# A decoder layer on one core: the residual and the row scaling ahead of the MLP moved to GpSimd

## The chip, the cores and the metric

The kernel runs on one core of a Trainium2 chip. The core has five engines with instruction queues of their own: TensorE (PE in the profile, with its weight loads as PEld), VectorE (DVE), ScalarE (ACT), GpSimd (POOL) and SyncE (SP), which issues most DMAs. Each engine works through its queue in order. An instruction that needs another engine's result waits for a semaphore, and everything behind it on its engine waits too. The metric is the device time of one launch in microseconds.

## The reference

One layer of a decoder, for a prompt of 256 tokens and for 8 samples of one token each, with 2048 channels in float32. Cut to the part around the change:

```python
x = x + gt1 * rmsnorm(out, p['g_post_mix'][l])          # the residual after the mixers

h2 = rmsnorm(x, p['g_pre_mlp'][l]) * (1.0 + sc2) + sh2  # input of the MLP
y2 = jnp.square(jax.nn.relu(h2 @ p['w_mlp_up'][l])) @ p['w_mlp_down'][l]
x = x + gt2 * rmsnorm(y2, p['g_post_mlp'][l])
```

`out` is the output projection of the three mixers (2048 by 2048). `w_mlp_up` is 2048 by 8192 and `w_mlp_down` 8192 by 2048. A row of `x` is one token, and both norms go over a row: each needs one factor per token. The kernel calls them `r1` (from the norm of `out`) and `r2` (from the norm of the new `x`).

## The kernel before

Every large product is computed in three passes (L602, L603, L604) over operands that are split into a high and a low part. `split` does this with a cast on ACT (L109) and a subtraction on DVE (L106), both for weights (`whi`, `wlo`) and for activations (`h2h`, `h2l`). The moving operand has 264 columns: 256 prompt tokens and 8 sample columns. Weights arrive as blocks of 128x1024 by SP's DMAs and are split up to two granules ahead of use.

The change lies at the seam between the output projection and the MLP. At this place the order of PE, DVE and ACT is written out by hand (`manual_schedule`, L1448); POOL's order there follows the order of the code. The steps, in order:

- `norms` and `rstd_sqrt` compute `r1` (ready at L199). `x1` holds the prompt's rows of the input, `og` the gated rows of `out`, as four tiles of 128x1024 each: two halves of tokens (`t`) by two halves of channels.
- POOL handles the samples' columns: two products (L1455, L1456), the residual of the samples (L1483, L1484), and their modulation (L1485, L1499, L1500) into `xa`.
- A chain of small 128x10 operations on DVE (L100, L1489, L103, L1492, L195 to L199) gives `r2` without forming the new rows first. From `r1` and `r2` come four diagonal matrices `dg` (L1497 on DVE, L1498 on ACT).
- The channels go into the MLP in four quarters of 512. `quad(0)` forms the first quarter on PE, by matmuls of the rows against `dg` (L1534, L1535), so that it needs no residual. `quad(1)` to `quad(3)` need the finished residual: `residual(q)` adds `r1*og` to `x1` in place on DVE (L1508, one 128x512 instruction for each `t`), ACT scales the rows by `r2` into two tiles named `gt` (L1515), and PE transposes them (L1532). `put_quad` then modulates the transposed quarter on DVE and ACT (L1545, L1547) and splits it (L109, L106).
- `begin_up` multiplies the quarters by the first 512 columns of `w_mlp_up`. After the granules for k = 0, 4 and 8 it issues `quad(1)`, `quad(2)` and `quad(3)`; after those for k = 2 and 6 it issues `residual(2)` and `residual(3)`, and at the end `residual(0)`. `residual(1)` stands right behind `quad(0)`. A granule here is 24 matmuls.
- The tiles `gt` have two buffers for all users. `dg` takes one of them, and each quarter's two scaled tiles take both.

Of the kernel before, what the change touches and what calls it, by code (L numbers as in the profile page):

```python
# [7 lines left out]
F32 = mybir.dt.float32  # L8
F32R = mybir.dt.float32r
I32 = mybir.dt.int32  # L10
AF = mybir.ActivationFunctionType
ALU = mybir.AluOpType
# [3 lines left out]
P = 128  # L16
D = 2048
KT = D // P
NP = 256
NS = 8  # L20
NT = NP + NS
# [36 lines left out]
def hybrid_step_kernel(  # L58
# [9 lines left out]
    V, S, T = nc.vector, nc.scalar, nc.tensor  # L68
# [13 lines left out]
    def nm(s):  # L82
        uid[0] += 1
        return f"{s}_{uid[0]}"

    def blk(shape=None, dt=F32):
        shape = shape or [P, 4, NT]
        return blkp.tile(shape, dt, tag="b", name=nm("b"))

    def sm(shape=None):  # L90
        return psm.tile(shape or [P, 512], F32, tag="sm", name=nm("sm"))

    def tmp(shape, tag, bufs=2):
        return tp.tile(shape, F32, tag=tag, name=nm(tag), bufs=bufs)
# [13 lines left out]
    def split(src, hi, lo):  # L108
        S.copy(hi, src)  # L109
        sub(lo, src, hi.bitcast(F32))  # L110

    order = tc.manual_schedule(engines={mybir.EngineType.PE, mybir.EngineType.SP, mybir.EngineType.Pool})
# [77 lines left out]
    def rstd_sqrt(ms, scale, out):  # L190

        n, w = out.shape
        xx, aa = tmp([P, 16], "sx")[0:n, 0:w], tmp([P, 16], "sa")[0:n, 0:w]
        S.activation(out, ms, AF.Sqrt, scale=scale, bias=eps)
        V.tensor_scalar(xx, ms, scale, EPS, ALU.mult, ALU.add)  # L195
        V.reciprocal(out, out)
        mul(aa, out, out)
        V.scalar_tensor_tensor(aa, aa, -0.5, xx, ALU.mult, ALU.mult)
        V.scalar_tensor_tensor(out, aa, 1.5, out, ALU.add, ALU.mult)  # L199
# [453 lines left out]
    def background():  # L653

        now[0] += 1
        while later and later[0][0] < now[0]:
            later.pop(0)[1]()
        bg.pump(rate[0])
        bs.pump(rate[1])
        wait = max([now[0] + 1 - AGE - x[0] for x in levels + samples] + [0])  # L660
        if wait and any(x[1][0].i == 2 for x in samples):
            wait += 2
        if rounds.due() and (wait or now[0] >= rounds.at + rounds.pace) or wait >= SLOT_WAIT:
            slot()
        rounds.tick()

    def new_acc():
        return pmm.tile([P, 2, 512], F32, tag="mm", name=nm("mm"))
# [229 lines left out]
    order = tc.manual_schedule(engines={mybir.EngineType.PE, mybir.EngineType.Pool})  # L898
# [460 lines left out]
    x1 = [[blk([P, 1024]) for _ in range(2)] for _ in range(2)]  # L1359
# [6 lines left out]
    def gated(m, src, Gv):  # L1366

        k = 2 * m
        sq = tmp([P, 2, NT], "vt")
        g = tmp([P, 2, NT], "gt")  # L1370
        if m < 7:
            S.activation(sq, src, AF.Square)
        else:
            S.activation(sq[:, 0, :], src[:, 0, :], AF.Square)
        V.tensor_scalar(g[:, 1, 0:NP], src[:, 1, 0:NP], Gv[:, k + 1, 0:1], None, ALU.mult)
        if m == 7:
            S.activation(sq[:, 1, :], src[:, 1, :], AF.Square)
        S.activation(g[:, 0, 0:NP], src[:, 0, 0:NP], AF.Copy, scale=Gv[:, k, 0:1])
        if m == 0:
            add(sqacc, sq[:, 0, :], sq[:, 1, :])  # L1380
        else:
            add(sqacc, sqacc, sq[:, 0, :])
            add(sqacc, sqacc, sq[:, 1, :])
        mul(gs[:, k:k + 2, :], src[:, :, NP:NT], Gv[:, k:k + 2, 1:NC])
        return g
# [26 lines left out]
    def norms():  # L1412

        ps = sm([P, 2 + NS])
        for t in range(2):
            T.matmul(ps[:, t:t + 1], sqacc[:, t * P:(t + 1) * P], ones[:, 0:1], start=True, stop=True)
        T.matmul(ps[:, 2:2 + NS], ones, sqacc[:, NP:NT], start=True, stop=True)
        r = tmp([P, 2 + NS], "nr", 1)
        rstd_sqrt(ps, 1.0 / D, r)
        return r  # L1420

    order = tc.manual_schedule(engines={mybir.EngineType.PE})
    order.__enter__()
    og = [[blk([P, 1024]) for _ in range(2)] for _ in range(2)]
# [20 lines left out]
    V.scalar_tensor_tensor(A2, mod[:, 4 * KT:5 * KT, :], 1.0, gpre2T.unsqueeze(2).to_broadcast([P, KT, NC]), ALU.add, ALU.mult)  # L1445
    B2 = mod[:, 3 * KT:4 * KT, :]
    order.__exit__(None, None, None)
    order = tc.manual_schedule(engines={mybir.EngineType.PE, mybir.EngineType.DVE, mybir.EngineType.Activation})  # L1448
    order.__enter__()
    Q = nc.gpsimd  # L1450
    rounds.steps(2)
    g = gated(7, z, G1)

    sp = tmp([P, 2, KT, NS], "os2", 1)
    Q.tensor_tensor(sp[:, 0], gs, xsT, op=ALU.mult)  # L1455
    Q.tensor_tensor(sp[:, 1], gs, gs, op=ALU.mult)  # L1456
    r1 = norms()

    pt = new_acc()
    for t in range(2):  # L1460
# [21 lines left out]
    xa = tmp([P, KT, NS], "xsn", 1)  # L1482
    Q.tensor_tensor(gs, gs, r1[:, 2:2 + NS].unsqueeze(1).to_broadcast([P, KT, NS]), op=ALU.mult)  # L1483
    Q.tensor_tensor(xsT, xsT, gs, op=ALU.add)  # L1484
    Q.tensor_tensor(xa, xsT, A2[:, :, 1:NC], op=ALU.mult)  # L1485

    q = tmp([P, 2 + NS], "rr", 1)
# [5 lines left out]
    r2 = tmp([P, 2 + NS], "rr0", 1)  # L1493
    rstd_sqrt(q, 1.0 / D, r2)
    dg = tmp([P, 4, P], "gt")
    for t in range(2):
        V.tensor_scalar(dg[:, t, :], ident, r2[:, t:t + 1], None, ALU.mult)  # L1497
        S.activation(dg[:, 2 + t, :], d1[:, t, :], AF.Copy, scale=r2[:, t:t + 1])  # L1498
    Q.tensor_tensor(xa, xa, r2[:, 2:2 + NS].unsqueeze(1).to_broadcast([P, KT, NS]), op=ALU.mult)  # L1499
    Q.tensor_tensor(xa, xa, B2[:, :, 1:NC], op=ALU.add)  # L1500
    h2h, h2l = [blk(dt=F32R) for _ in range(4)], [blk(dt=F32R) for _ in range(4)]

    def residual(q):

        cs = slice(q % 2 * 512, q % 2 * 512 + 512)
        for t in range(2):
            x = x1[t][q // 2][:, cs]
            V.scalar_tensor_tensor(x, og[t][q // 2][:, cs], r1[:, t:t + 1], x, ALU.mult, ALU.add)  # L1508

    def quad(q):  # L1510

        if q > 0:
            rows = [tmp([P, 4, P], "gt") for _ in range(2)]
            for t in range(2):
                S.activation(rows[t].rearrange("p k f -> p (k f)"), x1[t][q // 2][:, q % 2 * 512:q % 2 * 512 + 512], AF.Copy, scale=r2[:, t:t + 1])  # L1515
        hs, ls = (h[q][:, :, NP:NT] for h in (h2h, h2l))
        Q.tensor_copy(hs, xa[:, 4 * q:4 * q + 4, :])
        Q.tensor_tensor(ls, xa[:, 4 * q:4 * q + 4, :], hs.bitcast(F32), op=ALU.subtract)
        for i2 in range(2):
            if q > 0:  # L1520
                ps = sm([P, 2, NP])
            vt = tmp([P, 2, NT], "vt")
            for i in range(2):
                c0 = q % 2 * 512 + (2 * i2 + i) * P
                if q == 0:
                    pk = sm([P, NP])
                else:
                    pk = ps[:, i, :]
                for t in range(2):
                    o = pk[:, t * P:(t + 1) * P]  # L1530
                    if q > 0:
                        T.transpose(o, rows[t][:, 2 * i2 + i, :], ident)  # L1532
                    else:
                        T.matmul(o, x1[t][0][:, c0:c0 + P], dg[:, t, :], start=True, stop=False)  # L1534
                        T.matmul(o, og[t][0][:, c0:c0 + P], dg[:, 2 + t, :], start=False, stop=True)  # L1535
                if q == 0:
                    put_quad(q, i2, i, pk, vt)
            if q > 0:
                for i in range(2):
                    put_quad(q, i2, i, ps[:, i, :], vt)  # L1540

    def put_quad(q, i2, i, src, vt):
        k = 4 * q + 2 * i2 + i
        if i == 0 and (q == 0 or i2 == 0):
            V.tensor_scalar(vt[:, i, 0:NP], src, A2[:, k, 0:1], B2[:, k, 0:1], ALU.mult, ALU.add)  # L1545
        else:
            S.activation(vt[:, i, 0:NP], src, AF.Identity, scale=A2[:, k, 0:1], bias=B2[:, k, 0:1])  # L1547
        if q == 0 or i == 1:
            a = i if q == 0 else 0
            js = slice(2 * i2 + a, 2 * i2 + i + 1)  # L1550
            split(vt[:, a:i + 1, 0:NP], h2h[q][:, js, 0:NP], h2l[q][:, js, 0:NP])

    quad(0)
    residual(1)

    rate[:] = (0.0, 0.0)
    rounds.pace, rounds.batch = 5, 2
# [3 lines left out]
    def begin_up():  # L1561

        accs = [new_acc(), new_acc()]
        for k in range(0, KT, 2):
            granule(w_mlp_up[0], 0, 2, 0, 2 * CW, accs, h2H, h2L, k, k == 0, k + 2 == KT)
            if k % 4 == 0 and k + 4 < KT:
                quad(k // 4 + 1)
            elif k + 6 < KT:
                residual(k // 4 + 2)
            elif k + 2 == KT:  # L1570
                residual(0)
            if k >= 8:
                background()
        return [a[:, :, 0:NT] for a in accs]
# [47 lines left out]
    order = tc.manual_schedule(engines={mybir.EngineType.PE})  # L1622
# [99 lines left out]
```

## Time and profile before

| | |
|---|---|
| median of 3 runs | 1942.22 us (1941.23 to 1944.57) |
| span of the profiled execution | 1942.9 us, 42324 instructions |
| PE busy | 1903.4 us (98%) |
| PEld busy | 1812.1 us (93%) |
| DVE busy | 1186.1 us (61%) |
| ACT busy | 1006.5 us (52%) |
| POOL busy | 83.9 us (4%) |
| mean granted clock of PE | 0.994 |

The profile is one execution, and it gives the span from the first to the last instruction as that execution's own time; nothing outside the span is listed for it. The span is 0.7 us above the median of the three runs and inside their spread. Rows of the timeline begin with the start in us from the span's start and the duration in us; a bracket at the end names the idle time before the row and what ended it. Rows of the waits name who waited for whom: the sum in us, how often, and the longest.

### The profile page before, as it was taken

Reading aid. Unit: us, or ns where it says so; the run is one execution under the profiler, and the core shown is the slowest. Engines: PE = TensorE matmul, PEld = TensorE weight load, DVE = VectorE, ACT = ScalarE, POOL = GpSimd, SP = SyncE. Lnnn points to the kernel's source line nnn. Section 1 sums busy time; section 2 is a strip of 40 time slices with the busy share of each in tenths; the row PEclk is TensorE's granted clock in tenths of the full one; section 3 lists DMA queues with packets and bytes.
Section 4 is the critical chain, followed back from the end, with each engine's and each line's share of the span. In section 5 each row is a group of like instructions: output and inputs, shape, how many; then the busy total and the mean of one; then the engine's idle time right before and its main releaser. Section 6 shows DMA issues by size and latency. Waiting matters only on the chain.

```text
span 1942.9 us, 42324 instructions
## 1 busy us (share of the span) xinstructions
PE 1903.4 (98%) x17080; PEld 1812.1 (93%) x17080; DVE 1186.1 (61%) x2103; ACT 1006.5 (52%) x1825; POOL 83.9 (4%) x142
## 2 busy tenths in 40 slices
PE   6999999998999999999999999999999999999998
PEld 5989999988999998999999988999999999999997
DVE  4566667686578695565555666545556555555665
ACT  5444454665666765544444556444444545454444
POOL 1000000001001112200000010000000000000000
PEclk9999999999999999999999999999999999999999
DMA  9897786688588688987777846776566555555552
GB/s 317 299 337 247 249 287 213 214 250 276 175 262 290 214 258 283 306 266 249 253 256 233 300 129 195 229 226 199 178 182 184 179 180 184 177 183 182 179 183 99
DMA packets 339380, 442.06 MB, mean 228 GB/s; under 512 B 14930, under 2 KB 281024, under 8 KB 339184
## 3 DMA queue, kind: packets, MB, share of 16 engines
q1 hardware_dynamic: 329120, 409.62, 65.5%
q0 software_dynamic: 8992, 28.48, 4.6%
q8 instruction: 134, 2.20, 0.5%
q10 hardware_dynamic: 1072, 1.25, 0.2%
q14 instruction: 62, 0.51, 0.1%
HBM read 427.60 MB, written 11.70 MB: 226 GB/s over the span
## 4 chain that ended last, share of the span: by engine, by line
PE 95%; DMA 2%; issue 1%; ACT 1%; DVE 1%; POOL 0%; SPq 0%; ACTq 0%; DVEq 0%; POOLq 0%
PE mm L602 29%; PE mm L603 29%; PE mm L604 28%; PE ada L342 3%; PE ada L274 1%; PE sm L633 1%; PE sm L780 1%; DMA raw<-in_w_in_dram 1%; PE sm L640 0%; DMA b<-in_x_prompt_dram 0%; DMA vbc<-vs_d 0%; DVE wlo L106 0%; DMA b<-in_w_ada_dram 0%; ACT gt L1515 0%; PE sm L1176 0%
## 5 line engine op out<-in xcount | busy, mean ns | idle before, releaser
L602 PE MATMUL mm<-b,whi 128*128 128x264 f32 x4624 | 1326.6, 287 | 7.5 <-ACT b L109 3.5
L603 PE MATMUL mm<-b,whi 128*128 128x264 f32 x4624 | 1317.8, 285 | 0.8 <-DVE b L106 0.8
L604 PE MATMUL mm<-b,wlo 128*128 128x264 f32 x4624 | 1314.5, 284 | 1.4 <-issue 0.7
L106 DVE TENSOR_TENSOR wlo<-raw,whi 128x512 fp32r<-128x512 f32 x1136 | 775.5, 689 | 572.0 <-ACT whi L109 570.0
L109 ACT CAST whi<-raw 128x512 fp32r<-128x512 f32 x1136 | 695.4, 618 | 730.6 <-PE mm L603 654.5
L602 PEld LDWEIGHTS mm<-b,whi 128*128 128x128 f32 x4624 | 872.3, 189 | 49.1 <-issue 26.2
L604 PEld LDWEIGHTS mm<-b,wlo 128*128 128x128 f32 x4624 | 872.5, 189 | 2.2 <-DVE wlo L106 1.1
L603 PEld LDWEIGHTS mm<-b,whi 128*128 128x128 f32 x4624 | 872.2, 189 | 1.4 <-DVE b L106 1.3
L103 DVE TENSOR_TENSOR b<-b,mm 128x528 f32<-128x528 f32 (+1 forms) x137 | 95.7, 700 | 42.7 <-PE mm L604 42.7
L1057 DVE SCALAR_TENSOR_TENSOR st<-vbc,b,st 128x128 f32<-128x128 f32 (+1 forms) x96 | 34.1, 389 | 51.1 <-DMA vbc<-vs_d 44.2
L1055 ACT ACTIVATE st<-st,fs 128x128 f32<-128x128 f32 (+1 forms) x96 | 37.0, 430 | 53.0 <-DMA st<-in_state_hgrn_dram 27.0
L274 PE MATMUL ada<-b,cT 128*32 128x256 f32 (+1 forms) x640 | 35.7, 361 | 7.2 <-DMA b<-in_w_ada_dram 7.0
L342 PE MATMUL ada<-araw,cT 128*32 128x512 f32 x296 | 39.9, 601 | 0.0
L274 PEld LDWEIGHTS ada<-b,cT 128*32 128x32 f32 x640 | 18.2, 115 | 19.7 <-issue 6.4
L100 DVE TENSOR_TENSOR b<-b,b 128x512 f32<-128x512 f32 (+1 forms) x47 | 34.1, 740 | 1.4 <-ACT b L1165 0.9
L1058 POOL DMA_DIRECT2D out_dram<-st x32 | 23.5, 735 | 156.6 <-DVE st L1057 150.8
L342 PE MATMUL ada<-b,cT 128*32 128x512 f32 x216 | 26.2, 593 | 0.0
L106 DVE TENSOR_TENSOR b<-gt,b 128x528 fp32r<-128x528 f32 x32 | 22.7, 708 | 3.9 <-ACT whi L109 0.9
L106 DVE TENSOR_TENSOR b<-b 128x1024 f32<-128x1024 f32 (+1 forms) x24 | 24.3, 1016 | 0.0
L109 ACT CAST whi<-araw 128x512 fp32r<-128x512 f32 x20 | 12.4, 621 | 20.7 <-PE mm L603 19.0
L100 DVE TENSOR_TENSOR gt<-vt 128x528 f32<-128x528 f32 x32 | 22.4, 701 | 0.9 <-ACT vt L1581 0.9
L1587 ACT ACTIVATE b<-vt 128x528 fp32r<-128x528 f32 x32 | 20.7, 647 | 1.0
(339 smaller groups left out, 825.2 us busy)
## 6 DMA issues: line engine op xcount, KB each, us to landing
raw<-in_w_in_dram SPq DMA_DIRECT2D x232, 512.0 KB, 4.7
raw<-in_w_mlp_up_dram SPq DMA_DIRECT2D x128, 512.0 KB, 3.7
raw<-in_w_mlp_down_dram SPq DMA_DIRECT2D x128, 512.0 KB, 3.6
b<-in_w_ada_dram SPq DMA_DIRECT2D x102, 512.0 KB, 6.4
araw<-in_w_ada_dram SPq DMA_DIRECT2D x74, 512.0 KB, 6.0
raw<-in_w_branch_dram SPq DMA_DIRECT2D x48, 512.0 KB, 4.5
raw<-in_w_out_dram SPq DMA_DIRECT2D x32, 512.0 KB, 3.9
b<-in_w_ada_dram SPq DMA_DIRECT2D x32, 256.0 KB, 5.7
```

The source lines that it names most:

```text
L100: V.tensor_tensor(o, a, b, op=ALU.mult)
L103: V.tensor_tensor(o, a, b, op=ALU.add)
L106: V.tensor_tensor(o, a, b, op=ALU.subtract)
L109: S.copy(hi, src)
L274: T.matmul(acc[32 * j:32 * j + 32, 0:n], cT[:, k, :], w[:, n * j:n * j + n], start=k == 0, stop=k == KT - 1)
L342: T.matmul(self.acc[32 * j:32 * j + 32, :], cT[:, k, :], ws[j // 2][:, j % 2 * 512:j % 2 * 512 + 512], start=k == 0, stop=k == KT - 1)
L602: T.matmul(o, a, xh(k + j), start=first and j == 0, stop=False)
L603: T.matmul(o, a, xl(k + j), start=False, stop=False)
L604: T.matmul(o, b, xh(k + j), start=False, stop=last and j == n - 1)
L1055: S.activation(st[:, i, :], st[:, i, :], AF.Copy, scale=fs[:, h0 + i, b:b + 1])
L1057: V.scalar_tensor_tensor(st[:, i, :], v[:, i, :], k[:, h0 + i, NP + b:NP + b + 1], st[:, i, :], ALU.mult, ALU.add)
L1058: nc.gpsimd.dma_start(G.s_out(b, h0, nh), st)
```

## The change

The residual and the scaling by `r2` leave DVE and ACT for POOL. POOL's residual is two instructions for each `t` in place of one: `og` is multiplied by `r1` in place, then added to `x1`. The scaling has its own function `scaled(q)`, which fills the two `gt` tiles. POOL's order is now written out as well: `residual(1)` stands behind the two sample products, the split of the samples' columns (four casts, four subtractions) stands in one piece ahead of `quad(0)`, and then `scaled(1)`, `residual(2)`, `scaled(2)`, `residual(3)`, `scaled(3)`, `residual(0)`.

```diff
-    order = tc.manual_schedule(engines={mybir.EngineType.PE, mybir.EngineType.DVE, mybir.EngineType.Activation})
+    order = tc.manual_schedule(engines={mybir.EngineType.PE, mybir.EngineType.DVE, mybir.EngineType.Activation, mybir.EngineType.Pool})
...
+    def residual(q):
+
+        cs = slice(q % 2 * 512, q % 2 * 512 + 512)
+        for t in range(2):
+            x, o = x1[t][q // 2][:, cs], og[t][q // 2][:, cs]
+            Q.tensor_scalar(o, o, r1[:, t:t + 1], None, ALU.mult)
+            Q.tensor_tensor(x, x, o, op=ALU.add)
+
+    quad_rows = {}
+
+    def scaled(q):
+
+        quad_rows[q] = [tmp([P, 4, P], "gt") for _ in range(2)]
+        for t in range(2):
+            Q.tensor_scalar(quad_rows[q][t].rearrange("p k f -> p (k f)"), x1[t][q // 2][:, q % 2 * 512:q % 2 * 512 + 512], r2[:, t:t + 1], None, ALU.mult)
...
     r1 = norms()
+    residual(1)
...
-    def residual(q):
-
-        cs = slice(q % 2 * 512, q % 2 * 512 + 512)
-        for t in range(2):
-            x = x1[t][q // 2][:, cs]
-            V.scalar_tensor_tensor(x, og[t][q // 2][:, cs], r1[:, t:t + 1], x, ALU.mult, ALU.add)
-
     def quad(q):
 
-        if q > 0:
-            rows = [tmp([P, 4, P], "gt") for _ in range(2)]
-            for t in range(2):
-                S.activation(rows[t].rearrange("p k f -> p (k f)"), x1[t][q // 2][:, q % 2 * 512:q % 2 * 512 + 512], AF.Copy, scale=r2[:, t:t + 1])
-        hs, ls = (h[q][:, :, NP:NT] for h in (h2h, h2l))
-        Q.tensor_copy(hs, xa[:, 4 * q:4 * q + 4, :])
-        Q.tensor_tensor(ls, xa[:, 4 * q:4 * q + 4, :], hs.bitcast(F32), op=ALU.subtract)
+        rows = quad_rows.get(q)
...
+    for q in range(4):
+        hs, ls = (h[q][:, :, NP:NT] for h in (h2h, h2l))
+        Q.tensor_copy(hs, xa[:, 4 * q:4 * q + 4, :])
+        Q.tensor_tensor(ls, xa[:, 4 * q:4 * q + 4, :], hs.bitcast(F32), op=ALU.subtract)
     quad(0)
-    residual(1)
+    scaled(1)
+    residual(2)
...
             if k % 4 == 0 and k + 4 < KT:
                 quad(k // 4 + 1)
-            elif k + 6 < KT:
-                residual(k // 4 + 2)
-            elif k + 2 == KT:
-                residual(0)
+                if k < 8:
+                    scaled(k // 4 + 2)
+                    residual((k // 4 + 3) % 4)
```

POOL's queue before, from the samples' second product to the samples' last modulation (`nr` holds `r1`, `rr` holds `r2`, `xsn` is `xa`):

```order
L1456 TENSOR_TENSOR os_2445_15003<-gs_13718 128x128
L1483 TENSOR_TENSOR gs_13718<-gs_13718,nr_15010 128x128
L1484 TENSOR_TENSOR xsT<-xsT,gs_13718 128x128
L1485 TENSOR_TENSOR xsn_15054<-xsT,A_14980 128x128
L1499 TENSOR_TENSOR xsn_15054<-xsn_15054,rr_2456_15064 128x128
```

The same place on POOL with the change (`b_13709` and `b_13711` are tiles of `x1`, `b_13721` and `b_13723` tiles of `og`):

```order
L1473 TENSOR_TENSOR os_2445_15003<-gs_13718 128x128
L1457 TENSOR_SCALAR b_13721<-b_13721,nr_15010 128x512
L1458 TENSOR_TENSOR b_13709<-b_13709,b_13721 128x512
L1457 TENSOR_SCALAR b_13723<-b_13723,nr_15010 128x512
L1458 TENSOR_TENSOR b_13711<-b_13711,b_13723 128x512
L1501 TENSOR_TENSOR gs_13718<-gs_13718,nr_15010 128x128
L1502 TENSOR_TENSOR xsT<-xsT,gs_13718 128x128
L1503 TENSOR_TENSOR xsn_15058<-xsT,A_14980 128x128
L1517 TENSOR_TENSOR xsn_15058<-xsn_15058,rr_2456_15068 128x128
```

Four instructions of 128x512 now stand between `r1` and the rest of the samples' work, while DVE computes `r2`.

POOL's queue with the change behind the samples' last split, where the queue before ended (`gt` tiles are the scaled rows of quarters 1 and 2):

```order
L1561 TENSOR_TENSOR b_15091<-xsn_15058,b_15087 128x4x8
L1466 TENSOR_SCALAR gt_15134<-b_13709,rr_2456_15068 128x512
L1466 TENSOR_SCALAR gt_15135<-b_13711,rr_2456_15068 128x512
L1457 TENSOR_SCALAR b_13722<-b_13722,nr_15010 128x512
L1458 TENSOR_TENSOR b_13710<-b_13710,b_13722 128x512
L1457 TENSOR_SCALAR b_13724<-b_13724,nr_15010 128x512
L1458 TENSOR_TENSOR b_13712<-b_13712,b_13724 128x512
L1466 TENSOR_SCALAR gt_15203<-b_13710,rr_2456_15068 128x512
L1466 TENSOR_SCALAR gt_15204<-b_13712,rr_2456_15068 128x512
```

Each quarter's scaling is followed by the next quarter's residual, six instructions of 128x512 from one scaling to the next. PE's instructions stand in the same order as before.

ACT's queue before, from the split of a weight granule to the split of quarter 1:

```order
L109 CAST whi_15157<-raw_14910 128x512
L109 CAST whi_15161<-raw_14910 128x512
L1515 ACTIVATE gt_15167<-b_13709,rr_2456_15064 128x512
L1515 ACTIVATE gt_15168<-b_13711,rr_2456_15064 128x512
L1547 ACTIVATE vt_15174<-sm_15173,mod,A_14980 128x256
L109 CAST b_15081<-vt_15174 128x2x256
```

And with the change:

```order
L109 CAST whi_15173<-raw_14910 128x512
L109 CAST whi_15177<-raw_14910 128x512
L1552 ACTIVATE vt_15184<-sm_15183,mod,A_14980 128x256
L109 CAST b_15085<-vt_15184 128x2x256
L1552 ACTIVATE vt_15194<-sm_15193,mod,A_14980 128x256 x2
```

The two scalings that stood behind two weight casts are gone from ACT; in the same way DVE loses its eight L1508 and keeps everything else in the old order, but for one pair of neighbours that change places after the seam.

## The prediction

> **What bounds the kernel now.** I read the page first, then the seam in windows, then who waits for whom there.
>
> ```profile
> PE 1903.4 (98%) x17080; PEld 1812.1 (93%) x17080; DVE 1186.1 (61%) x2103; ACT 1006.5 (52%) x1825; POOL 83.9 (4%) x142
> 1154.60:1161.20 6.60, 6.60 (x56) 6.53 (x56) 3.80 (x9) 3.54 (x9) 2.54 (x10) 1.00 0.01 4
> 1161.20:1187.20 26.00, 21.51 (x170) 20.38 (x169) 16.16 (x26) 18.74 (x33) 0.00 (x0) 1.00 0.34 102
> 1187.20:1240.00 52.80, 52.80 (x435) 51.22 (x434) 31.75 (x48) 27.34 (x46) 0.00 (x0) 1.00 0.75 236
> ```
>
> The columns of a window are its length, then the busy time of PE, PEld, DVE, ACT and POOL. PE is busy 98% of the span, so only PE's idle time can be won. PE is full before (1154.6 to 1161.2) and after (from 1187.2), and idle 26.00 - 21.51 = 4.49 us in between. Since PE is full behind the seam, what is won or lost here reaches the end unchanged.
>
> ```profile
> PEld sm L1532 <- ACT gt L1515: 5.7, 6, 1.4
> PE sm L1532 <- ACT gt L1515: 4.5, 6, 1.2
> 1161.06 0.28 PE L604 MATMUL mm<-b,wlo 128*128 128x264 f32 x1
> 1162.55 0.33 PE L1532 MATMUL sm<-cst,gt 128*128 128x128 f32 x1 [1.22 <-ACT gt L1515]
> 1163.17 0.98 PE L1532 MATMUL sm<-cst,gt 128*128 128x128 f32 x7 [0.28 <-ACT gt L1515]
> 1163.90 0.37 PE L602 MATMUL mm<-b,whi 128*128 128x264 f32 x1
> ...
> 1166.82 0.28 PE L604 MATMUL mm<-b,wlo 128*128 128x264 f32 x1
> 1171.21 0.33 PE L1532 MATMUL sm<-cst,gt 128*128 128x128 f32 x1 [1.21 <-ACT gt L1515]
> 1892.53 0.87 PE sm L780 x8
> ```
>
> The waits are six, all of PE's transposes (L1532) on ACT's scaled rows (L1515), two for each of `quad(1)` to `quad(3)`. The 24 matmuls of a granule start between 1163.90 and 1166.82, 0.12 us apart. So at 1161.18 PE was ready for the transposes of `quad(1)`, and it was done with them at 1163.90: 2.72 us. Eight transposes that wait for nothing take 0.87 (the L780 row of the chain). That leaves 1.85 us lost at each quarter, 5.55 at three; the two rows of the waits say 4.5 and 5.7. I take **5.5 us** as all that can be won. A quarter's period is 1171.21 - 1162.55 = 8.66 now and 8.66 - 1.85 = 6.81 without its waits.
>
> **What is removed.**
>
> ```profile
> 1160.53 1.35 ACT L109 CAST whi<-raw 128x512 fp32r<-128x512 f32 x2 [0.61 <-PE mm L603]
> 1161.78 1.33 ACT L1515 ACTIVATE gt<-b,rr 128x512 f32<-128x512 f32 x2
> 1160.29 1.41 DVE L1508 SCALAR_TENSOR_TENSOR b<-b,nr,b 128x512 f32<-128x512 f32 x2
> 1161.62 1.29 DVE L106 TENSOR_TENSOR wlo<-raw,whi 128x512 fp32r<-128x512 f32 x2
> 1165.58 0.69 DVE L106 TENSOR_TENSOR b<-vt,b 128x512 fp32r<-128x512 f32 x1 [1.28 <-ACT b L109]
> ```
>
> ACT's scaling starts late because it is queued behind two weight casts that wait for PE to free their buffers. With it gone from ACT the wait goes away, if POOL has the rows in time: -5.5. DVE's eight L1508 (0.7 us each) were on nobody's path; nothing waits for them but L1515, so their removal alone is worth nothing.
>
> **What POOL's new work costs by itself.** POOL has done no 128x512 operation before; its nearest rows are these.
>
> ```profile
> L936 POOL MEMSET att<- 128x1024 f32 x1 | 1.0, 955 | 0.0
> 1150.48 0.43 POOL L1483 TENSOR_TENSOR gs<-gs,nr 128x128 f32<-128x128 f32 x1 [1.33 <-DVE nr L199]
> 1150.99 0.46 POOL L1484 TENSOR_TENSOR xsT<-xsT,gs 128x128 f32<-128x128 f32 x1
> 1154.32 0.47 POOL L1499 TENSOR_TENSOR xsn<-xsn,rr 128x128 f32<-128x128 f32 x1 [2.36 <-DVE rr L199]
> 1155.36 0.21 POOL L1517 CAST b<-xsn 128x32 fp32r<-128x32 f32 x1
> 1155.65 0.25 POOL L1518 TENSOR_TENSOR b<-xsn,b 128x32 fp32r<-128x32 f32 x1
> 1156.81 0.46 POOL L1517 CAST b<-xsn 128x32 fp32r<-128x32 f32 x1
> 1157.36 0.25 POOL L1518 TENSOR_TENSOR b<-xsn,b 128x32 fp32r<-128x32 f32 x1
> ```
>
> A TENSOR_TENSOR goes from 0.25 us at 32 columns to about 0.45 at 128: 2.1 ns a column, so 0.45 + 384 x 0.0021 = **1.25 us** at 512. The Trainium skill, page "GPSIMD Engine Reference", section 3.1, has 4497 ns for 2048 columns; a quarter of it would be an estimate of 1.12 us, which the two rows here bear out. A TENSOR_SCALAR reads one stream, not two. Its lower end is the memset, which only writes: about 0.1 + 512 x 0.00083 = 0.53. Its upper end is the TENSOR_TENSOR, 1.25. I take **0.70**, nearer the memset, since one stream is added to it. Between dependent POOL instructions lie 0.07 (1150.48 + 0.43 to 1150.99). So a residual is 2 x 0.77 + 2 x 1.32 = 4.2 us, a scaling 1.5, and one quarter on POOL 5.7, which is under the 6.81 that PE needs. Alone, POOL would keep up.
>
> **What POOL and DVE do to each other.** Three of the four casts take 0.21 us; the one at 1156.81 takes 0.46, and it runs beside a DVE operation of two SBUF inputs that began at 1156.78. In the other direction, of the two equal L1497 on DVE (from SBUF to SBUF, with one input) one takes 0.29 and one 0.46, and the pair ends 0.08 after POOL's L1499, which began at 1154.32, just behind the first of them.
>
> ```profile
> 1151.98 0.17 DVE L100 TENSOR_TENSOR rr<-fs,nr 128x10 f32<-128x10 f32 x1
> 1152.19 0.17 DVE L1489 SCALAR_TENSOR_TENSOR rr<-fs,rr 128x10 f32<-128x10 f32 x1
> 1152.39 0.17 DVE L100 TENSOR_TENSOR rr<-rr,nr 128x10 f32<-128x10 f32 x1
> 1152.60 0.17 DVE L103 TENSOR_TENSOR rr<-rr,xx 128x10 f32<-128x10 f32 x1
> 1152.80 0.17 DVE L1492 TENSOR_SCALAR rr<-rr 128x10 f32<-128x10 f32 x1
> 1154.21 0.66 DVE L1497 TENSOR_SCALAR gt<-cst,rr 128x128 f32<-128x128 f32 x2
> L1497 DVE TENSOR_SCALAR gt<-cst,rr x2: 287/373/459, 1154.2 to 1154.4; 128x128 f32<-128x128 f32 x2
> 1156.78 0.43 DVE L106 TENSOR_TENSOR b<-vt,b 128x256 fp32r<-128x256 f32 x1 [0.47 <-ACT b L109]
> 1154.60 0.46 PE L1534 MATMUL sm<-gt,b 128*128 128x128 f32 x2 [0.74 <-PE ada L342]
> ```
>
> So I forecast that a POOL operation that reads SBUF and a DVE operation of these kinds take turns: whichever comes second waits for the first. The Trainium skill states this as a rule (page "SBUF — State Buffer", section "Who interferes with whom"): a DVE instruction with two SBUF inputs and a GpSimd instruction that reads SBUF exclude each other for a whole instruction. By that rule the change pays for its move; the two pairs of rows above agree with it in both directions.
>
> *First place, the chain of `r2`.* `residual(1)` starts when `r1` is there, at 1150.48: TENSOR_SCALAR to 1151.18, TENSOR_TENSOR to 1152.50, TENSOR_SCALAR to about 1153.35, TENSOR_TENSOR to about 1154.75, with the samples' L1501 to 1155.35 behind it. DVE's small operations each have two SBUF inputs and come one at a time, each needing the one before, so one slips in after each POOL instruction: the one at 1151.98 goes at 1152.50, that of 1152.19 at 1153.35, that of 1152.39 at 1154.75, that of 1152.60 at 1155.35. That is +2.75 there, and 2.75 to 3.15 for what follows. Behind this chain stand the diagonals L1497 and PE's L1534, which started at 1154.60 with PE idle before it; nothing covers the delay. I take **+3.0** (0 without contention).
>
> *Second place, the three quarters.* The samples' work keeps its place behind `r2`. Before, POOL was free at 1157.36 + 0.25 = 1157.61; now at 1160.6. `scaled(1)` takes 1.5 and half a microsecond of DVE: 1162.65. PE wants it at 1161.18 + 3.0 = 1164.18, so it is early by 1.5. From there `scaled(3)` is two quarters of POOL's work away. In a quarter's period DVE has four `wlo` (2 x 1.29) and two `b` (2 x 0.69), 3.96 us, all with two SBUF inputs. How much of this POOL loses: the slow cast lost 0.25 beside an operation of 0.43, a share of 0.58, which is 2.3; at most all 4.0. So a quarter is 5.7 + 2.3 = 8.0 to 9.7 against 6.81, and two are 2.4 to 5.8 too long. Less the 1.5, `scaled(3)` is late by 0.9 to 4.3; I take **+2.4**, nearer the measured share.
>
> *Third place, the split of a quarter.* `h2l` for k = 4 was ready at 1165.58 + 0.69 = 1166.27, and PE wanted it 0.12 after 1166.82: 0.67 to spare. A POOL TENSOR_TENSOR in front can hold that DVE operation up to 1.25. I put 0.3 at each quarter, **+0.9** (0 to 1.8).
>
> *At nothing:* the eight sample splits in one piece need no more time than before, and their first columns are due only at the end of `quad(0)`, 3.6 us of PE work behind the diagonals. `residual(0)` feeds only the kernel's end. DMA is at a share of 0.34 in the window, and SP's queue is untouched.
>
> **Sum:** -5.5 + 3.0 + 2.4 + 0.9 = +0.8. Against the span of 1942.9 that is 1943.7; against the median of 1942.2, 0.7 below the span, **1943.0**. With the bounds of the terms: -5.5 + 2.75 + 0.9 + 0 = -1.9 to -5.5 + 3.15 + 4.3 + 1.8 = +3.8, so 1940.3 to 1946.0 for this case alone.
>
> **The rivals.**
>
> *They overlap freely (0.20).* Then `residual(1)` ends at 1150.48 + 4.2, the samples' columns are split within `quad(0)`, POOL's 5.7 stays under 6.81, and the three late terms vanish: -5.5, 1936.7. With a TENSOR_SCALAR as dear as a TENSOR_TENSOR a quarter is 7.9, and about 4 come back: 1940.7. For it speaks that two spans on POOL are thin evidence; against it, that both directions show the same.
>
> *POOL becomes the bound, and the kernel slower (0.27).* The place is the six POOL instructions between two scalings, four of them TENSOR_SCALARs, and the price is that of one. At 1.25 each the `r2` chain is +4.0, a quarter 7.9 + 2.3 = 10.2, and two of them 6.8 too long with 0.4 to spare at `scaled(1)`: -5.5 + 4.0 + 6.4 + 0.9 = +5.8, 1948.0. Between 0.70 and 1.25 the sum rises by 5.0, 9.1 for each microsecond, so it passes +3.9 at about 1.04. Above 1.25 it goes on: 1.6 gives +9. For it speaks that no TENSOR_SCALAR on POOL is in the trace; against it, that one stream ought not to cost as much as two.
>
> *The wait only changes its name (0.03).* Something else (the split of a quarter, the weight casts) is late at the same point, and the time stays at 1942.
>
> **How the numbers follow.** My case holds 0.50. A measurement of this kernel can tell about 0.2%, 3.9 us, from no change. Of my case's 0.50, 0.44 lies within that and 0.06 beyond it on the slow side. Of the free overlap's 0.20, 0.15 is faster by more and 0.05 within. Of POOL's 0.27, 0.25 is slower and 0.02 within; the last 0.03 is within. Together: faster 0.15, same 0.54, slower 0.31. The range reaches down to the free overlap, 1936.5, and up to 1949.5, past POOL's 1948.0; above it are left about 0.12 and below it about 0.05.
>
> **What would show it.** In the profile after: PE's start of `quad(0)`'s first matmul, 1154.60 now, near 1157.6 (1154.6 if I am wrong about the chain); the 128x10 rows on DVE spread over some 4 us in place of 1; transposes of `quad(1)` without a wait and those of `quad(3)` waiting for POOL; 128x512 rows on POOL near 0.70 and 1.25; DVE's `wlo` and `b` longer than 0.69 beside them. A TENSOR_SCALAR above 1.04, or PE waiting nowhere between 1154 and 1187, would make the forecast wrong.

## The result: slower by 0.4%

The changed kernel takes 1950.77 us in the median of 4 runs (1949.45 to 1954.22), the kernel before 1943.39 (4 runs, 1941.23 to 1945.34). The ratio is 1.0039, with an interval of 1.0026 to 1.0053: 7.4 us more, where 1943.0 with a range up to 1949.5 had been forecast. The profiled execution took 1949.45 us, of which 1947.7 are its span.

These are the page's first line and three windows of the kernel after, the same stretches of time as before. The columns of a window are its length, the busy time of PE, PEld, DVE, ACT and POOL, then the granted clock and the DMA share with its rate.

```profile
PE 1903.9 (98%) x17080; PEld 1813.8 (93%) x17080; DVE 1190.8 (61%) x2095; ACT 1003.5 (52%) x1819; POOL 120.0 (6%) x164
1154.60:1161.20 6.60, 6.23 (x30) 6.26 (x31) 2.40 (x6) 1.99 (x6) 4.93 (x13) 0.52 0.00 0
1161.20:1187.20 26.00, 20.61 (x153) 19.34 (x153) 16.47 (x19) 13.44 (x25) 25.01 (x15) 0.95 0.34 103
1187.20:1240.00 52.80, 52.80 (x431) 51.22 (x431) 31.41 (x46) 28.10 (x48) 3.69 (x3) 0.99 0.68 216
```

Two things leap out. POOL, idle in the second window before, is busy for 25.01 of 26.00 us. And in the first window PE's granted clock is 0.52; before it was 1.00, and PE did 56 matmuls there where it now does 30. PE's busy time hides this: 6.23 of 6.60 us look full. The 0.95 of the second window, 1.00 before, is a second and shorter loss of the clock near its end.

The waits at the seam after the change, and PE's rows at the same places that were shown of before:

```profile
PE sm L1537 <- POOL gt L1466: 4.0, 3, 2.3
PE sm L1539 <- issue: 3.7, 1, 3.7
PE mm L603 <- DVE b L106: 1.2, 1, 1.2
1154.97 0.77 PE L1539 MATMUL sm<-gt,b 128*128 128x128 f32 x2 [3.70 <-issue]
1155.53 0.64 PE L1540 MATMUL sm<-gt,b 128*128 128x128 f32 x2
...
1161.01 0.39 PE L1539 MATMUL sm<-gt,b 128*128 128x128 f32 x2
1161.38 0.37 PE L602 MATMUL mm<-b,whi 128*128 128x264 f32 x1
1164.39 1.03 PE L1537 MATMUL sm<-cst,gt 128*128 128x128 f32 x8
1173.84 0.98 PE L1537 MATMUL sm<-cst,gt 128*128 128x128 f32 x7 [0.48 <-POOL gt L1466]
1184.74 1.72 PE L1537 MATMUL sm<-cst,gt 128*128 128x128 f32 x7 [1.21 <-POOL gt L1466]
```

The six waits on ACT's rows are gone; in their place PE waits 3.7 us ahead of `quad(0)` and 4.0 for POOL. A pair of `quad(0)`'s matmuls takes 0.64 us while the clock is at half and 0.39 at the end, when it is back. At `quad(3)` the same seven transposes take 1.72 us where they took 0.98 at `quad(2)`: the clock is at half there again.

Since the stretch ahead of the seam differs by some microseconds from one execution to the next, the seam gets a ruler of its own: from the start of POOL's first sample product (1148.33 before, 1145.75 after) to the start of ACT's first Relu (1188.88 and 1194.68). It is **40.55 us before and 48.93 after**. Cut at PE's milestones, worked out from such rows:

| step on PE | before | after | difference |
|---|---|---|---|
| samples' first product to `quad(0)` (the chain) | 6.27 | 9.22 | +2.95 |
| `quad(0)` | 3.56 | 6.41 | +2.85 |
| first granule and transposes of `quad(1)` | 5.74 | 3.80 | -1.94 |
| to the granule behind `quad(2)` | 8.67 | 9.40 | +0.73 |
| to the granule behind `quad(3)` | 8.67 | 11.53 | +2.86 |
| to the first Relu | 7.64 | 8.57 | +0.93 |

The gain that was hoped for shows at `quad(1)` alone. The last row needs no wait to be longer: its first matmuls still run at half clock. POOL's rows of the kernel after:

```profile
1148.01 1.57 POOL L1457 TENSOR_SCALAR b<-b,nr 128x512 f32<-128x512 f32 x1 [1.45 <-ACT gt L1397]
1149.66 1.28 POOL L1458 TENSOR_TENSOR b<-b,b 128x512 f32<-128x512 f32 x1
1150.92 1.56 POOL L1457 TENSOR_SCALAR b<-b,nr 128x512 f32<-128x512 f32 x1
1166.23 2.00 POOL L1457 TENSOR_SCALAR b<-b,nr 128x512 f32<-128x512 f32 x1
1168.32 1.26 POOL L1458 TENSOR_TENSOR b<-b,b 128x512 f32<-128x512 f32 x1
1169.56 4.22 POOL L1466 TENSOR_SCALAR gt<-b,rr 128x512 f32<-128x512 f32 x2
1180.61 4.07 POOL L1466 TENSOR_SCALAR gt<-b,rr 128x512 f32<-128x512 f32 x2
L1458 POOL TENSOR_TENSOR b<-b,b 128x512 f32<-128x512 f32 x8 | 10.3, 1290 | 0.7
```

The TENSOR_TENSOR costs 1.28, as forecast (1.25). The TENSOR_SCALAR costs **1.57 alone** and 2.0 to 2.1 beside DVE's splits, more than twice the 0.70 that was taken and above the 1.25 that was its upper end. DVE's rows in the chain of `r2`, which took 0.17 each before:

```profile
1149.81 1.16 DVE L100 TENSOR_TENSOR rr<-rr,nr 128x10 f32<-128x10 f32 x1
1151.00 0.63 DVE L103 TENSOR_TENSOR rr<-rr,xx 128x10 f32<-128x10 f32 x1
1151.87 0.64 DVE L195 TENSOR_SCALAR sx<-rr 128x10 f32<-128x10 f32 x1
1152.77 1.12 DVE L198 SCALAR_TENSOR_TENSOR sa<-sa,sx 128x10 f32<-128x10 f32 x1
```

The first of them began at 1149.81 and ended at 1150.97, POOL's addition ran from 1149.66 to 1150.94: an operation on ten columns stood until the one on 512 was over. The second, from 1151.00, fell into POOL's TENSOR_SCALAR of 1150.92 to 1152.48 and stood as well, but only to 1151.63. The third, of one operand, ended at 1152.51, when the TENSOR_SCALAR did; in the run with 28 extra matmuls below it took its 0.17 there.

### The profile page after: what moved, and what is told of

Its sections match the earlier page's. It is cut to its first block, busy times and chain, and to the rows that moved or that the text cites. A ratio compares the mean times of both kernels' runs of the same rounds, so it can differ in the third digit from the quotient of the medians.

```text
span 1947.7 us, 42337 instructions
## 1 busy us (share of the span) xinstructions
PE 1903.9 (98%) x17080; PEld 1813.8 (93%) x17080; DVE 1190.8 (61%) x2095; ACT 1003.5 (52%) x1819; POOL 120.0 (6%) x164
## 3 DMA queue, kind: packets, MB, share of 16 engines
q10 hardware_dynamic: 1072, 1.25, 0.2%
## 4 chain that ended last, share of the span: by engine, by line
PE 94%; DMA 2%; DVE 1%; POOL 1%; ACT 1%; issue 1%; SPq 0%; DVEq 0%; ACTq 0%; POOLq 0%
PE mm L602 29%; PE mm L603 28%; PE mm L604 28%; PE ada L342 3%; PE ada L274 1%; PE sm L633 1%; PE sm L780 1%; DMA raw<-in_w_in_dram 1%; DMA b<-in_w_ada_dram 1%; DMA st<-in_state_gla_dram 1%; DMA st<-in_state_hgrn_dram 0%; PE sm L640 0%; DMA b<-in_x_prompt_dram 0%; POOL gt L1466 0%; DVE wlo L106 0%
## 5 line engine op out<-in xcount | busy, mean ns | idle before, releaser
L106 DVE TENSOR_TENSOR wlo<-raw,whi 128x512 fp32r<-128x512 f32 x1136 | 780.1, 693 | 576.2 <-ACT whi L109 573.8
L106 DVE TENSOR_TENSOR b<-gt,b 128x528 fp32r<-128x528 f32 x32 | 22.7, 709 | 3.3
L106 DVE TENSOR_TENSOR b<-b 128x1024 f32<-128x1024 f32 (+1 forms) x24 | 24.4, 1020 | 0.0
```

The lines of the kernel that those rows point to most:

```text
L106: V.tensor_tensor(o, a, b, op=ALU.subtract)
```

## The experiments

Theory A: four causes add up. POOL's instructions hold up the chain of `r2`; PE idles for that and loses half its clock in `quad(0)`; POOL's own pace (10.4 us from one scaling to the next, 1163.33 to 1173.77) is longer than PE's quarter; against them stands a gain by the order. Rival B puts the low clock down to POOL's work, not to PE's idling. Other rivals make one of the causes the whole loss. All runs are measured by the seam, in one profile each, as well as by the time. A is the changed kernel, B the kernel before.

**PE kept busy while it waits.** On A:

```diff
     rounds.steps(3)
+    fill = sm([P, P])
+    for i in range(28):
+        T.matmul(fill, ident, ident, start=i == 0, stop=i == 27)
```

> The changed kernel with 28 extra 128x128 matmuls on PE in the stretch where it waits for r2 (their result is read by nobody). The ruler of all these runs is the seam: from the start of POOL's first sample product to the start of ACT's first Relu, 40.55 us before and 48.93 with the change. Theory A (PE's clock falls because PE idles 3.7 us ahead of quad(0)): the idle is under 1 us, the granted clock stays at 1.0, quad(0) takes about 3.6 us in place of 6.4. Since POOL paces what follows, only the 1.6 us for which POOL's second scaling had waited for PE come back: seam about 47.3. Rival B (the clock falls because of POOL's work, whatever PE does): clock 0.5 and quad(0) 6.4 us again, seam 48.9.

The size was wrong: 28 matmuls became 56 PE instructions and took 6.52 us, so `quad(0)` started 11.81 us into the seam in place of 9.22. The clock stayed at 1.00 through `quad(0)`, which took 3.49; at `quad(3)`, behind a wait of 2.27 us for POOL, it was at half for 6.83 us. Seam 49.38; the time, 1.0047 of before (1.0029 to 1.0065), says nothing on the price. The same with 13:

> The run with extra matmuls again, with 13 of them in place of 28: in the run before each became two PE instructions, so that they took 6.5 us and themselves made quad(0) 2.6 us late. 13 take 3.0 us and end before r2. Theory A (idle PE loses its clock): PE idles under 1 us, clock 1.0, quad(0) 3.5 us from 9.2 us behind the seam's start, POOL's second scaling starts 1.6 us earlier than with the change, and POOL paces the rest: seam about 47.3. Rival B (POOL's work lowers the clock): quad(0) 5 to 6.4, seam 48 to 49.

PE's rows of this run, the third from `quad(3)`, and POOL's last scaling:

```profile
1156.81 0.46 PE L1542 MATMUL sm<-gt,b 128*128 128x128 f32 x2 [0.60 <-PE sm L1495]
1160.23 0.39 PE L1543 MATMUL sm<-gt,b 128*128 128x128 f32 x2
1185.00 0.98 PE L1540 MATMUL sm<-cst,gt 128*128 128x128 f32 x7 [1.21 <-POOL gt L1466]
1180.88 4.07 POOL L1466 TENSOR_SCALAR gt<-b,rr 128x512 f32<-128x512 f32 x2
```

`quad(0)` starts at 9.23 as with the change and takes 3.56 at clock 1.00, with POOL's work untouched. Rival B falls. Seam **45.80**, 3.13 less than with the change, where 1.6 had been expected. POOL's last scaling ends 1.56 us sooner (37.37 us into the seam, 38.93 with the change), since its second scaling no longer waits for PE: `quad(0)` holds the buffer of the `gt` tile that it fills. That part was foreseen. The other 1.57 us lie behind the last scaling (8.43 us to the Relu, 10.00 with the change). There the change runs `quad(3)` at half clock, its seven transposes in 1.72 us; here they take 0.98. This run loses the clock a second time as well, but at `quad(2)`, for 3.41 us, and there PE has to wait for POOL again afterwards, so it costs nothing. Where the second loss falls was not foreseen. The time, 1.0034 of before (1.0021 to 1.0047), cannot be told from the change's 1.0039.

**The chain late without POOL.** On B, 14 times, then 7:

```diff
     V.tensor_scalar(q, q, 0.0, None, ALU.max)
+    for _ in range(14):
+        V.tensor_scalar(q, q, 1.0, None, ALU.mult)
```

> The kernel before, with 14 extra multiplications by 1.0 on DVE (128x10, 0.2 us each) in the chain of r2, and nothing on POOL. Theory A: r2 is 2.9 us late, PE idles 3.6 us, its clock is granted at 0.5 for some 6 us and quad(0) takes 6.4 us in place of 3.6: seam 40.55 + 2.9 + 2.9 = 46.3. Rival B: clock 1.0 throughout, seam 43.4.

> The kernel before with 7 extra small multiplications on DVE in the chain of r2 in place of 14: PE idles about 0.7 + 1.5 = 2.2 us ahead of quad(0) (3.64 with 14). If PE loses its clock only after an idle stretch longer than this, quad(0) stays at 3.6 us and the granted clock at 1.0: seam 40.55 + 1.45 = 42.0. Rival (every longer idle costs clock): quad(0) 4.5 us or more, seam 43 or more.

The first PE rows of `quad(0)` in the two, 14 first:

```profile
1157.23 0.76 PE L1536 MATMUL sm<-gt,b 128*128 128x128 f32 x2 [3.64 <-issue]
1157.78 0.63 PE L1537 MATMUL sm<-gt,b 128*128 128x128 f32 x2
```

```profile
1157.85 0.76 PE L1536 MATMUL sm<-gt,b 128*128 128x128 f32 x2 [2.19 <-issue]
```

With none of the moved work on POOL the clock over `quad(0)` is 0.68 in both, and `quad(0)` takes 5.09 and 5.12 us. It takes no 6.4, because the clock is at half for 3.41 us here and for 6.83 with the change. Seams 44.95 and 43.52; times 1.0028 (1.0018 to 1.0037) and 1.0011 (1.0001 to 1.0021). The idling is the cause. My expectation for the shorter delay was wrong: 2.19 us of idling lost the clock as 3.64 did.

**The first residual back on DVE.** On A, behind the diagonals; the other three stay on POOL:

```diff
     r1 = norms()
-    residual(1)
...
+        if q == 1:
+            for t in range(2):
+                x = x1[t][q // 2][:, cs]
+                V.scalar_tensor_tensor(x, og[t][q // 2][:, cs], r1[:, t:t + 1], x, ALU.mult, ALU.add)
+            return
...
         S.activation(dg[:, 2 + t, :], d1[:, t, :], AF.Copy, scale=r2[:, t:t + 1])
+    residual(1)
```

> The changed kernel with residual(1) alone given back to DVE, behind the diagonals; the rest stays on POOL. If POOL's four instructions make the r2 chain late by taking turns with DVE, that chain is back at 6.3 us from the samples' first product to quad(0) (9.2 with the change), the clock stays at 1.0 and quad(0) takes 3.6. What is left is POOL's pace, 10.4 to 10.9 us for a quarter in place of 6.8: PE's transposes of quad(2) and quad(3) wait for POOL, seam about 44.2, 3.7 above before. Rival (the chain and the clock are the whole loss, POOL's pace is none): seam about 35 to 37.

Chain 6.27, `quad(0)` 3.56 at clock 1.00: both are as before. Seam **42.80**, 1.4 less than expected, and the whole loss ahead of the first granule is due to four POOL instructions. PE still waits for POOL:

```profile
PE sm L1542 <- POOL gt L1471: 5.5, 5, 2.2
```

At `quad(2)`, behind waits of 2.16 and 1.37 us, the clock is at half for 3.41 us. POOL stands idle nowhere in this stretch and sets the pace, so that loss does not reach the end. Time 1.0024 (1.0015 to 1.0034).

**One half of the change alone.** On A with the residual as DVE's one instruction (the first two lines, for all quarters, and `residual(1)` behind the diagonals as in the run before), only the scaling stays on POOL. With the last two lines instead, the scaling is on ACT and only the residual stays on POOL, where the change has it.

```diff
+            x = x1[t][q // 2][:, cs]
+            V.scalar_tensor_tensor(x, og[t][q // 2][:, cs], r1[:, t:t + 1], x, ALU.mult, ALU.add)
...
-            Q.tensor_scalar(quad_rows[q][t].rearrange("p k f -> p (k f)"), x1[t][q // 2][:, q % 2 * 512:q % 2 * 512 + 512], r2[:, t:t + 1], None, ALU.mult)
+            S.activation(quad_rows[q][t].rearrange("p k f -> p (k f)"), x1[t][q // 2][:, q % 2 * 512:q % 2 * 512 + 512], AF.Copy, scale=r2[:, t:t + 1])
```

> Only the scaling is on POOL; the residual is DVE's single instruction, residual(1) behind the diagonals. POOL then has two multiplications a quarter, 3.2 us alone and 4.1 beside DVE, under the 6.8 to 7.7 that PE takes for a quarter. If the pace of POOL was what made the third part of the loss, PE waits nowhere for POOL: chain 6.3, quad(0) 3.6, seam 36.5 to 38.5, as with neither on POOL (37.8). Rival (taking turns with DVE makes the splits late even so): seam above 39.

> Only the residual is on POOL, residual(1) still ahead of the r2 chain's end as in the change; the scaling is on ACT straight behind the quarter before. The chain of r2 stays at 9.2 us and PE's clock at half through quad(0) (5 to 6.4 us); a quarter's residual is 6 to 6.5 us on POOL, just under PE's quarter, so PE does not wait for it: seam about 37.8 + 2.9 + 1.5 to 2.9 = 42.2 to 43.6. Rival (contention with DVE stretches it past PE's quarter): 44 to 47.

Scaling alone on POOL, its rows for `quad(1)` and `quad(2)` and the one wait that is left on it:

```profile
1153.08 3.31 POOL L1465 TENSOR_SCALAR gt<-b,rr 128x512 f32<-128x512 f32 x2
1157.48 3.74 POOL L1465 TENSOR_SCALAR gt<-b,rr 128x512 f32<-128x512 f32 x2 [1.09 <-PE sm L1536]
PE sm L1536 <- POOL gt L1465: 0.2, 1, 0.2
```

POOL now waits for PE (1.09), not PE for POOL. Seam **37.77**, time 0.9981 of before (0.9969 to 0.9993). Residual alone on POOL: chain 9.22, clock 0.70, `quad(0)` 5.01, no wait on POOL at the quarters, seam 43.52, time 1.0022 (1.0009 to 1.0035). Both came out as expected: the scaling alone may sit on POOL; the residual ahead of `r2` may not, and not because POOL lacks the time for it.

**Neither on POOL, in the change's order.** Both edits above together.

> The changed kernel's order with its operations on the old engines: residual on DVE as one instruction, scaling on ACT, but each placed where the change has it (scaling of a quarter straight behind the quarter before it, so ahead of ACT's weight casts; residual(1) behind the diagonals). If the 5.5 us that could be won were a matter of order and not of engines, the six waits of PE's transposes are gone: seam 35 to 36, 5 us below before. Rival (the quarter's split or the weight casts are late instead): seam 39 to 41, the waits under another name.

The waits of PE at the seam:

```profile
PE mm L603 <- DVE b L106: 1.1, 3, 0.4
PE sm L1536 <- ACT gt L1465: 0.3, 1, 0.3
```

Seam **37.77**, equal to that with the scaling on POOL; time 0.9982 (0.9973 to 0.9992). So the gain does come from the order. But it is 2.78 us, not 5.5: each quarter's split is now the last thing late.

**The multiplications as TENSOR_TENSOR.** On A, all ten, with the factor spread over 512 columns:

```diff
-            Q.tensor_scalar(o, o, r1[:, t:t + 1], None, ALU.mult)
+            Q.tensor_tensor(o, o, r1[:, t:t + 1].to_broadcast([P, 512]), op=ALU.mult)
```

> The change with POOL's ten multiplications by a factor per row written as TENSOR_TENSOR with the factor spread over the 512 columns. If their 1.56 us belongs to TENSOR_SCALAR as an operation on POOL, each takes 1.28 like the addition: a quarter on POOL is 1.1 us shorter, twice, and the chain 0.3 to 0.5: seam about 46. Rival (the product or the factor per row costs it, in either form): 1.5 or more each, seam 48.5 to 50.

The first multiplication and addition on POOL, three rows of `quad(0)` on PE, and PE's longest wait for another engine at the seam:

```profile
1152.72 1.04 POOL L1457 TENSOR_TENSOR b<-b,nr 128x512 f32<-128x512 f32 x1 [1.42 <-PE ada L342]
1153.84 1.28 POOL L1458 TENSOR_TENSOR b<-b,b 128x512 f32<-128x512 f32 x1
1159.78 0.46 PE L1539 MATMUL sm<-gt,b 128*128 128x128 f32 x2 [3.77 <-issue]
1160.97 0.39 PE L1540 MATMUL sm<-gt,b 128*128 128x128 f32 x2
1161.58 0.64 PE L1540 MATMUL sm<-gt,b 128*128 128x128 f32 x2
PE mm L602 <- ACT b L109: 3.6, 3, 2.6
```

The multiplication costs 1.04 alone, less than the addition and a third less than TENSOR_SCALAR. Yet the chain stays at 9.29: three of DVE's 128x10 operations now take 1.00, 0.96 and 1.12 us, each until a POOL instruction is over. At the quarters PE waits for the splits in place of POOL. Seam 47.40, 1.53 less than with the change; `quad(0)`, at clock 0.67, takes 5.19 in place of 6.41, which is 1.22 of it. What the cheaper form itself is worth is not shown, since both runs lose the clock twice, at different places. Time 1.0043 (1.0030 to 1.0056).

**The first residual behind the samples.** On A, all still on POOL:

```diff
     r1 = norms()
-    residual(1)
...
+    residual(1)
     quad(0)
     scaled(1)
```

> The change with residual(1) moved behind the samples' split in POOL's queue, everything else on POOL as in the change. The chain of r2 is free of POOL's long instructions: 6.3 us, clock 1.0, quad(0) 3.6. But scaled(1) now starts after a residual that begins only 9.3 us behind the seam's start: it is ready at about 18.5 to 19.5 where PE wants it at 12.8, so PE idles some 6 us there, and may lose its clock behind that. POOL's pace of 10.5 to 11 a quarter follows: seam 49 to 51, no better than the change. Rival (the late chain is the main loss): seam 46 or less.

Chain 6.26, `quad(0)` 3.57, clock 1.00; then, in PE's rows:

```profile
1166.07 0.47 PE L1536 MATMUL sm<-cst,gt 128*128 128x128 f32 x1 [4.14 <-POOL gt L1466]
1167.61 1.76 PE L1536 MATMUL sm<-cst,gt 128*128 128x128 f32 x7 [1.07 <-POOL gt L1466]
```

The window 1166 to 1170 is granted 0.50. The idling moved to `quad(1)`, and the clock went there too (and once more at `quad(3)`). Seam 49.47, time 1.0051 (1.0037 to 1.0066).

**A finer split.** On the run with neither on POOL:

```diff
-        if q == 0 or i == 1:
-            a = i if q == 0 else 0
+        if q == 0 or i2 == 0 or i == 1:
+            a = i if q == 0 or i2 == 0 else 0
```

> As the run with neither operation on POOL, and the first half of each later quarter is split in two pieces of 128x256 (as quad(0) is), so that its first channels are ready sooner. With neither on POOL the seam came to 37.8 and not to 35 because PE waits for DVE's and ACT's split of the quarter, 0.3 to 0.9 us each time. If that is the last thing late, those waits shrink: seam 36.5 to 37.3, 0.5 to 1.3 us less. Rival (four more instructions a quarter make it later): seam 38 or more.

Seam 37.00, as expected, and the wait on `b L106` is gone from the list. The time, 0.9982 (0.9972 to 0.9992), cannot tell it from the run without: 0.8 us lies within the intervals. The three versions at 0.998 lie 3.6 to 4.8 us below the kernel before, each in the medians of its own comparison, and so beat both kernels.

## Why the prediction was wrong, step by step

The runs put the seam together, step by step: 40.55 before; -2.78 by the order (37.77, the same with the scaling on POOL); +5.03 by the residual of the later quarters on POOL as well (42.80); +3.00 by `residual(1)` in the chain, with PE kept busy (45.80); +3.13 by PE's clock (48.93).

| step | forecast | measured |
|---|---|---|
| what the order can win | -5.5 | -2.78 |
| the chain of `r2` | +3.0 | +3.00 |
| POOL's pace at the quarters | +2.4 | +5.03, the split with it |
| the split of a quarter | +0.9 | within the line above |
| PE's clock in `quad(0)`, and POOL's wait for it | none | +1.56 |
| PE's clock at `quad(3)` | none | +1.57 |
| sum | +0.8 | +8.38 |

Each measured size is that of one profile. The times have the same signs, but not everywhere the same sizes: `residual(1)` back on DVE takes the ratio from 1.0039 to 1.0024, about 3 us, where the seam says 6.13, and that run's interval, 2.9 to 6.6 us above before, does not hold its seam's 2.25. What lies between is not shown.

*The chain* was right, in place and in size, though the size had help from two errors: the TENSOR_SCALAR was longer than taken, and held DVE up less than I let it. DVE did not slip in just one operation behind each POOL instruction: its addition at 1151.00 was through 0.85 us before POOL's TENSOR_SCALAR was, and the next operation, at 1151.66, which reads one operand, took 0.17 inside the same instruction, while the two at 1149.81 and 1152.77 stood through a TENSOR_TENSOR. With both multiplications a third shorter, but as TENSOR_TENSOR, the chain stayed at 9.29. That POOL and DVE take turns was read from the right rows; that the second always waits for the whole of the first holds for the TENSOR_TENSOR here and not for the TENSOR_SCALAR.

*POOL's pace* failed by the size of one term: the TENSOR_SCALAR, taken at 0.70 and measured at 1.57. The six instructions of a quarter come to 4 x 1.57 + 2 x 1.28 = 8.84 us without their gaps, where 5.3 was taken. Two quarters measured 10.44 and 10.89, so the gaps and DVE add 1.6 to 2.05, no more than the 2.3 that was allowed for DVE. It takes both halves of the change to overfill POOL: the scaling alone costs nothing at the quarters, the residual alone 1.35 us (below). The upper end was set at the TENSOR_TENSOR on the reasoning that one stream cannot cost more than two. The runs show the opposite. The rival "POOL becomes the bound" named the place, and the point (1.04) from which it decides; its own price stopped at 1.25, and its remark that 1.6 would give +9 is close to the +7.4 measured, but partly by chance, since it left out the clock and counted on 5.5.

*The ceiling* failed in its reasoning: all of PE's waits on L1515 were counted as winnable. The split of a quarter was seen to have 0.67 us to spare, but the weight splits in front of it on DVE were not moved up with PE. PE 1.85 us earlier against 0.67 to spare leaves 1.18 short at a quarter. In the run with neither on POOL, PE waits for `b L106` in their place, and 2.72 of the 5.5 us are lost again.

*The split of a quarter* was a right term, though small beside POOL's pace. In the change, DVE's two weight splits ahead of the split of `quad(1)` take 2.41 us beside POOL, where such a pair took 1.29 before:

```profile
1164.39 2.41 DVE L106 TENSOR_TENSOR wlo<-raw,whi 128x512 fp32r<-128x512 f32 x2 [1.27 <-ACT whi L109]
```

PE's wait for `b L106` at `quad(1)` is 1.24 us with the change and 0.32 with neither on POOL; at `quad(2)` and `quad(3)` POOL's pace covers it. With the residual alone on POOL, where PE never waits for POOL at the quarters, the seam is 43.52 - 37.77 = 5.75 longer than with neither; the chain has 2.96 of it, `quad(0)` 1.44, and 1.35 is left at the quarters.

*PE's clock* was left out. The forecast let PE idle 3 us longer and priced only the idling. What it does to the clock was in no row of the kernel before at this place, where PE idled 0.74 and its clock was 1.00. The changed kernel around its two losses:

```profile
1150.68:1154.09 3.41, 0.59 (x8) 0.00 (x0) 3.18 (x8) 0.30 (x1) 3.33 (x4) 1.00 0.00 0
1154.09:1157.50 3.41, 2.53 (x12) 2.56 (x13) 1.38 (x4) 0.69 (x2) 2.87 (x10) 0.50 0.00 0
1157.50:1160.92 3.42, 3.42 (x18) 3.42 (x18) 1.40 (x4) 1.37 (x3) 2.50 (x5) 0.50 0.00 0
1181.40:1184.81 3.41, 0.40 (x2) 0.21 (x3) 1.41 (x2) 0.05 (x1) 3.41 (x3) 1.00 0.55 167
1184.81:1188.22 3.41, 3.41 (x16) 3.41 (x17) 1.24 (x2) 1.97 (x4) 3.33 (x3) 0.50 0.47 146
```

At the seam of the profiles here the clock was at half twelve times, nine times for 3.41 us and three times for 6.83, twice as long. Where one profile has two losses, they start 30.72, 23.90 and 23.89 us apart: 9, 7 and 7 times 3.41. So the clock changes on a grid of 3.41 us. In the 3.41 us ahead of each loss PE had idled for 1.79 to 3.41 us (2.82 and 3.01 in the first and fourth row). Other such stretches at full clock, with up to 1.49 us of idling and in one case 1.81, left it alone. The clock stayed at half for a second stretch where PE idled for 0.88 us or more in the first (second row), and came back where it idled for 0.37 or less.

The Trainium skill has it (page "TensorE: Matmul & The Clock Gate", Part 1): an idle window of about 3.4 us halves PE's clock, and a busy one restores it, with windows that run freely. By that rule the forecast of 3.0 us more would have had a term of 1.7 to 3.4 us as an estimate, for one window or two at half speed. The runs agree in the halving, in its cause and in windows that run freely. They do not agree that the idling must fill a window: about 2 us within one were enough, as in the run with 7 multiplications (2.04).

So the size of this term hangs on where the windows lie in an execution: `quad(0)` is 1.4 to 2.9 us longer in the profiles here. In the run with TENSOR_TENSOR the clock fell only 1.4 us after PE had resumed (0.39 a pair at 1160.97, 0.64 at 1161.58), when the next window began. And a loss counts only where no later wait for POOL covers it: of the 2.85 us in `quad(0)`, 1.56 reached the end, while the loss at `quad(3)`, behind POOL's last scaling, did so with 1.57.

The chance of 0.31 for slower by more than 0.2% went to what happened. The range ended 1.3 us too low.

## What to carry to other kernels

When work moves to an engine that has not yet run such an operation, the neighbours bound its price poorly: measure the one instruction first, since here one form cost 1.57 us and another form of the same product 1.04. A delay on the way to TensorE costs more than its length if TensorE idles in it for about two microseconds or more. A few matmuls that nobody reads kept the clock in one stretch here; that they shorten the whole launch is not shown. Look at the granted clock in short windows over the whole stretch, not only where a loss is expected: the second loss came behind a wait for POOL. Before a wait is counted as a gain, follow the next operand behind it: half of these 5.5 us were already owed to something else, and the part that was left came from the order, on any engine.

## What the runs showed of the hardware

- On GpSimd a TENSOR_SCALAR of 128x512 in float32 takes 1.57 us and a TENSOR_TENSOR 1.28; the TENSOR_TENSOR whose second operand is one column spread over 512 takes 1.04. Beside VectorE's splits these become 1.7 to 2.1, 1.3 to 1.7 and 1.2 to 1.5.
- VectorE's 128x10 operations of two operands rose from 0.17 to as much as 1.22 us beside a GpSimd TENSOR_TENSOR and ended with it. One that began 0.08 us into a TENSOR_SCALAR of 1.56 took 0.63 and was done 0.85 before it, much the same in four profiles. What makes the difference was not tried.
- TensorE's granted clock fell to 0.5 for 3.41 or 6.83 us, twelve times in nine profiles, on a grid of 3.41 us, each time behind a stretch of the grid in which TensorE had idled for 1.79 us or more. At 1.49 or less it stayed at 1.00; where between the two it turns was not tried, and one stretch with 1.81 kept it.
